# A two-layer mixer in one kernel: Newton's steps on GpSimd, two weight loads moved ahead, block sums moved back

## The chip, the cores and the metric

The kernel runs on one core of a Trainium2 chip. Its engines are TensorE (PE in the profile; its weight loads are PEld), VectorE (DVE), ScalarE (ACT), GpSimd (POOL) and SyncE (SP), which issues most of the DMAs. Each engine works through its own queue in order, and semaphores tie the queues together. The metric is the device time of one execution in microseconds (us); three runs are shown, and the execution that was profiled has a time of its own.

## The reference

```python
D_MODEL, SEQ, CHUNK = 1024, 512, 64          # batch 1, float32, 8 heads of 128
# layer 0: gated linear recurrence (HGRN2) and squared-ReLU MLP; then a shared K/V projection
# layer 1: differential attention over that K/V and squared-ReLU MLP
def rms_norm(x, w):
    y = xf * lax.rsqrt(jnp.mean(xf * xf, axis=-1, keepdims=True) + EPS)
    return (y * w).astype(x.dtype)
def hgrn2_mixer(h, w_in, lb, gate_norm_w, w_out):        # h is rms_norm(x, a_norm_pre)
    proj = h @ w_in
    q, f, i, g = jnp.split(proj, ...)                    # 1024 columns each
    ...                                                  # q, k and log_f from q and f, per head
    o = hgrn2_recurrence(q, k, log_f, i)                 # chunks of 64 frames
    o = rms_norm(o, gate_norm_w) * jax.nn.silu(g)
    return o.reshape(B, S, D_MODEL) @ w_out
```

All that the change touches lies in the HGRN2 mixer, the first 290 us of 1271: the statistics 1/rms of x (512 numbers), the projections q and f (per head), i (the "values") and g (the "gates"), the recurrence, the norm of each head's output and the projection by `w_out`.

## The kernel before

Activations lie transposed, features on the 128 partitions and 512 frames along the row. Every large product is made of three matmuls in a short format: an operand is split into `hi` (a rounded copy, made by ACT) and `lo` (the rest, made by DVE as raw minus hi), and PE adds hi·hi, hi·lo and lo·hi. So each weight block passes through a DMA into a `raw` buffer (tag `raw`, 4 buffers), an ACT copy (`whi_…`) and a DVE subtraction (`wlo_…`; 8 buffers each) before PE can use it. In the tiles' names `qf` is a head's q and f columns, `wi`/`i` the first half of the values, `wg`/`g` the first pair of gates, `gs` and `is` the later gates and values, which are computed from sums of blocks (seven products in place of eight), `ao` the output projection.

`split_w` does the splitting with ACT and DVE. `split_d` leaves DVE out: ACT writes hi and minus raw, and a DMA issued by POOL adds the raw weights onto the latter in memory (`accum_op`), so `wlo` then comes from a DMA. Heads 0 to 3 take the first way (`load_w`), heads 4 to 7 the second (`load_d`).

The statistics: ACT squares x (`sqx`), DVE adds the four squares, PE sums over the partitions (`ps_mc`, 16 small matmuls), and `rsqrt_col` makes 1/sqrt of the 128x4 result `rcol`: `nx` = mean + eps, a first guess by integer arithmetic, and three Newton steps of three instructions each on tiles of 128x4 (`nt`, `rcol`). Then `nrcol`, the diagonal matrix `dg`, and PE's product `ps_sp`, which spreads the 512 numbers over the partitions; DVE copies it to `rb`, with which every gate is scaled. Head 0 and head 1 wait for `rb`.

`block_sums` makes four sums and differences of halves of the normalised input (tiles `sums`, then `whi_x`, `wlo_x`, and the last into `uhi`, `ulo`), which the later gates and values need (first at `gs_x`, 116 us). Its first step is eight ACT copies of x, scaled, into `sums` (L720), each 128x256.

The first projections follow one another on PE: head 0's and head 1's q and f, the values (`i`, four tiles of 512 columns), the first gates (`g`), heads 2 and 3, and so on. `head` runs beside them: gates, then seven levels of the recurrence, in which two to four heads alternate between a few small matmuls (`gl`), DVE multiplications (L849, L850) and a masked copy (L825), then state (`st`), output (`o`), `head_norm` (squares, `rsqrt_col`, scaling into `os_a`, four transposes `hn_a` on PE) and `store_u`.

What sets the order: PE's queue is the order in which the Python generators issue its instructions. `Plan` keeps a planned time, which each matmul advances; a chain such as `head` yields planned delays (the `W_…` numbers: `W_HEAD` between a head's norm and its transposes) or conditions, and is resumed when these are over; the main chain fills the time between. The queues of the other engines are arranged by the framework's scheduler by what is ready and by priority, within the dependences; `tc.issue_after` holds instructions behind a given one.

Of the kernel before, what the change touches and what calls it, by code (L numbers as in the profile page):

```python
# [13 lines left out]
AF = mybir.ActivationFunctionType  # L14
# [3 lines left out]
P = 128  # L18
# [15 lines left out]
W_KEYS, W_STATE = 1.5, 0.8  # L34
W_HEAD, W_STORE = 11.7, 5.5
W_QK, W_NEXT, W_P, W_PER_TILE, W_PT = 3.6, 0.94, 5.0, 0.66, 2.5
# [52 lines left out]
def trunk_kernel(ctx: ExitStack, tc: tile.TileContext, x_t, w_qf, w_g, w_gs, w_i, w_is, w_ao, w_kv, w_q, w_bo, w_up, w_us, w_dn,  # L89
# [73 lines left out]

    last_split = []

# [37 lines left out]

    def load_d(src, ncols, name):

        out = []
        per = 1024 // ncols
        for pr in range(ncols // 128):
            out += split_d(fetch_w(src, ncols, pr, name), src[:, per * pr:per * (pr + 1), :], f"{name}_{pr}")
        return out  # L210
# [28 lines left out]

    def rsqrt_col(ms, add, out, scale=1.0):  # L240

        n = ms.shape[1]
        x = cp.tile([P, 4], F32, tag="nx", name="nx", bufs=4)[:, :n]
        t = cp.tile([P, 4], F32, tag="nt", name="nt", bufs=4)[:, :n]
        if isinstance(add, float):
            v.tensor_scalar(x, ms, scale, add, op0=ALU.mult, op1=ALU.add)
        else:
            v.scalar_tensor_tensor(x, ms, scale, add, op0=ALU.mult, op1=ALU.add)
        v.tensor_scalar(out.bitcast(I32), x.bitcast(I32), -0.5, 1597463007.0, op0=ALU.mult, op1=ALU.add)
        for _ in range(3):  # L250
            v.scalar_tensor_tensor(t, out, -0.5, out, op0=ALU.mult, op1=ALU.mult)
            v.tensor_tensor(t, t, x, op=ALU.mult)
            v.scalar_tensor_tensor(out, t, 1.5, out, op0=ALU.add, op1=ALU.mult)

# [366 lines left out]

    def head_norm(pool, po, add, name):

# [6 lines left out]
        for c in range(4):  # L630
            if c % 2 == 0:
                v.tensor_scalar(os[:, c, :], po[:, c * P:(c + 1) * P], y[:, c:c + 1], None, op0=ALU.mult)
            else:
                a.activation(os[:, c, :], po[:, c * P:(c + 1) * P], AF.Copy, scale=y[:, c:c + 1])
        yield W_HEAD
        pt = smt(f"hn_{name}")
# [58 lines left out]
    def block_sums(xs, ts):  # L695

        gain = gn[:, G_APRE:G_APRE + 8]
        e, f = sums

        def split(src, sign, n):  # L700
            if n < 3:
# [16 lines left out]
        for r in range(4):  # L718
            for n, t in enumerate((e, f)):
                a.activation(t[:, r], xs[2 * r][:, n * 256:n * 256 + 256], AF.Copy, scale=gain[:, 2 * r:2 * r + 1])  # L720
            yield 2.0
        v.tensor_tensor(e, e, f, op=ALU.subtract)
        split(e, 1.0, 0)
        yield 5.0
        odd(1, f, ALU.subtract)
        split(f, 1.0, 1)
        yield 5.0
        odd(1, e, ALU.add)
        split(e, -1.0, 2)
        yield 5.0  # L730
        odd(0, e, ALU.subtract)
        split(e, -1.0, 3)

    def start(hp, xs, maskf):
# [14 lines left out]
        yield W_XSUM  # L749
        rsqrt_col(mean_cols([ssum[:, j, :] for j in range(2)], S, onesd), EPS, rcol)  # L750
        v.tensor_scalar(nrcol, rcol, -1.0, None, op0=ALU.mult)
# [40 lines left out]
    def hgrn(hp, w0, xs):  # L792
# [8 lines left out]
        def head(h, pss):  # L801
            if h < 2:
# [10 lines left out]
                            tf.rearrange("p (c t) -> p c t", c=4), op=ALU.mult)  # L813
            a.activation(qc[:, :, P:192], qq.rearrange("p (c b two) -> p c b two", c=4, two=2)[:, :, :, 1], AF.Copy)
            yield W_GATE if h >= 2 else W_GATE_FIRST
# [74 lines left out]
            done(("po", h))  # L890
            for pt in head_norm(hp, po, EPS, f"a{h}"):
                if isinstance(pt, float):
                    yield pt
# [131 lines left out]
        for p in range(4):  # L1025
            for h in (2 * p, 2 * p + 1):
                if h >= 3 and h % 2:
                    yield until(("rec", h - 3))
                wt = w0 if h == 0 else w1 if h == 1 else load_w(w_qf[h], 256, None, f"qf{h}") if h < 4 else load_d(w_qf[h], 256, f"qf{h}")
                pss = [mmt(f"qf{h}_{n}") for n in range(2)]  # L1030
# [13 lines left out]
            if p == 0:  # L1044
                wv = load_w(w_i, 512, None, "wi")
                vts[0], vts[1] = [hp.tile([P, 4, 256], F32, tag="vt", name=f"vt{i}", bufs=3) for i in range(2)]
                for tt in range(4):

                    ps = (smt if tt < 2 else mmt)(f"i{tt}")
                    for kt in range(8):  # L1050
                        xmm(ps, wv, kt, 512, tt * P, kt == 0, kt == 7)
                        yield 0
                    if tt == 0:
                        yield until("rcol")
                    for i in range(2):
                        a.activation(vts[i][:, tt, :], ps[:, i * 256:(i + 1) * 256], AF.Copy, scale=rcol[:, tt:tt + 1])
                yield until("rb")
                spawn(block_sums(xs, ts), 2.0)
                wt = load_w(w_g, 256, None, "wg")
                for j in range(2):  # L1060
# [48 lines left out]
    def attention(ap, f):  # L1109
# [27 lines left out]
        def unit(h, qi, kq, vt, bt, po, mx):  # L1137
# [40 lines left out]
            if qi == 3:  # L1178

                ez = col("ez")  # L1180
                v.scalar_tensor_tensor(ez, mx[:, :, 2], EPS, mx[:, :, 2], op0=ALU.mult, op1=ALU.mult)
                for hn in head_norm(ap, po, ez, f"b{h}"):
                    if isinstance(hn, float):
                        yield hn
                store_u(h, hn)
                yield W_STORE
                done(("amix", h))
# [166 lines left out]
```

## Time and profile before

| | |
|---|---|
| three runs | 1271.01, 1273.31, 1273.58 us; median 1273.31 |
| the profiled execution | 1273.18 us, span on the core 1271.4 us |
| PE busy | 1240.0 us, 98% of the span |
| DVE, ACT, POOL busy | 825.8, 673.9, 95.6 us |
| DMA | 158.54 MB, mean 125 GB/s |
| chain that ended last | PE 79%, DMA 6%, issue 6%, DVE 5%, ACT 4% |

A page of the profile gives busy time by engine, then the span in slices, the DMA queues, the chain that ended last, and the costliest groups of instructions. The sum of the prediction is made against the profiled execution, 1273.18 us, which lies 0.13 us under the median. With PE at 98%, what is to be read is where PE stands still, and for whom.

### The profile page before, as it was taken

The numbers are of one execution on the slowest core, as the hardware profiler recorded it, in microseconds if no ns is written. First come the engines' busy times: TensorE is split into PE (matmuls) and PEld (weight loads), VectorE is DVE, ScalarE is ACT, GpSimd is POOL, SyncE is SP. The second block draws the span as 40 slices with busy tenths as digits, with TensorE's granted clock in tenths as the row PEclk, the third lists the DMA queues.
The fourth block names the chain that finished last, engine by engine and source line by source line (L and its number), as shares of the span: only waits on it lengthen the run. The fifth ranks groups of instructions, "written<-read, shape, count | busy, mean of one in ns | idle before, by whom it ended". The sixth has DMA issues, their size and how long they took to land.

```text
span 1271.4 us, 21443 instructions
## 1 busy us (share of the span) xinstructions
PE 1240.0 (98%) x8440; PEld 1122.8 (88%) x8440; DVE 825.8 (65%) x1654; ACT 673.9 (53%) x1248; POOL 95.6 (8%) x166
## 2 busy tenths in 40 slices
PE   9999999999999999999999999999999999999996
PEld 7788898899988988989999787889998898988996
DVE  7768885866854654636488978664885463663645
ACT  7345546437751733715556877664773371561632
POOL 0102211210000000000100000001000000000000
PEclk9999999999999999999999999999999999999999
DMA  7223557342356663644616322313435355363521
GB/s 253 72 67 92 122 115 184 94 150 68 135 166 124 179 149 95 186 106 115 217 51 203 113 88 79 100 63 105 137 111 158 96 175 122 103 196 74 158 102 67
DMA packets 57303, 158.54 MB, mean 125 GB/s; under 512 B 6354, under 2 KB 8659, under 8 KB 57203
## 3 DMA queue, kind: packets, MB, share of 16 engines
q1 hardware_dynamic: 45920, 120.34, 30.2%
q0 software_dynamic: 11040, 36.71, 13.7%
q8 instruction: 66, 1.08, 0.4%
q14 instruction: 35, 0.28, 0.1%
q10 hardware_dynamic: 242, 0.13, 0.0%
HBM read 147.45 MB, written 9.70 MB: 124 GB/s over the span
## 4 chain that ended last, share of the span: by engine, by line
PE 79%; issue 6%; DMA 6%; DVE 5%; ACT 4%; POOL 0%; SPq 0%; DVEq 0%; ACTq 0%; POOLq 0%
PE dn L114 20%; PE qf L114 7%; PE up L114 7%; PE ux L114 6%; PE kq L114 6%; PE ao_h L114 3%; DMA raw_s<-in_w_us_dram 3%; PE bo_h L114 3%; PE dn_h L114 3%; PE uz L114 3%; PE gl L114 3%; PE v L114 3%; PE g L114 2%; PE lg L114 2%; PE i L114 2%
## 5 line engine op out<-in xcount | busy, mean ns | idle before, releaser
L114 PE MATMUL dn<-uhi,whi_dn 128*128 128x512 f32 x384 | 151.9, 396 | 0.0
L114 PE MATMUL dn<-ulo,whi_dn 128*128 128x512 f32 x384 | 151.9, 396 | 0.0
L114 PE MATMUL dn<-uhi,wlo_dn 128*128 128x512 f32 x384 | 151.9, 395 | 0.0
L200 ACT ACTIVATE whi_a<-raw_a 128x1024 fp32r<-128x1024 f32 x24 | 25.4, 1059 | 118.5 <-PE dn L114 115.6
L114 PEld LDWEIGHTS dn<-uhi,whi_dn 128*128 128x128 f32 x384 | 72.2, 188 | 17.8 <-ACT r L563 0.7
L114 PEld LDWEIGHTS dn<-uhi,wlo_dn 128*128 128x128 f32 x384 | 72.2, 188 | 17.3
L114 PEld LDWEIGHTS dn<-ulo,whi_dn 128*128 128x128 f32 x384 | 72.2, 188 | 16.9
L173 DVE TENSOR_TENSOR wlo_dn<-raw_dn,whi_dn 128x1024 fp32r<-128x1024 f32 x64 | 76.6, 1220 | 5.9 <-ACT whi_dn L172 4.6
L468 DVE TENSOR_TENSOR ulo<-r,uhi 128x1024 fp32r<-128x1024 f32 (+1 forms) x40 | 40.2, 1010 | 53.7 <-ACT uhi L467 53.7
L114 PE MATMUL up<-xhi,wlo_up 128*128 128x256 f32 x256 | 72.1, 281 | 1.0 <-DVE wlo_up L173 1.0
L114 PE MATMUL up<-xhi,whi_up 128*128 128x256 f32 x256 | 72.6, 284 | 0.0
L114 PE MATMUL up<-xlo,whi_up 128*128 128x256 f32 x256 | 71.8, 281 | 0.0
L172 ACT ACTIVATE whi_dn<-raw_dn 128x1024 fp32r<-128x1024 f32 x64 | 65.7, 1051 | 7.1 <-PE up L114 3.0
L114 PE MATMUL dn_h<-uhi,whi_dn 128*128 128x256 f32 x240 | 66.6, 278 | 0.0
L114 PE MATMUL dn_h<-ulo,whi_dn 128*128 128x256 f32 x240 | 66.3, 276 | 0.0
L114 PE MATMUL dn_h<-uhi,wlo_dn 128*128 128x256 f32 x240 | 66.3, 276 | 0.0
L610 DVE TENSOR_TENSOR zacc<-dn,zacc 128x512 f32<-128x512 f32 x32 | 22.1, 691 | 59.1 <-PE dn L114 59.0
L512 POOL DMA_DIRECT2D raw_s<-in_w_us_dram x24 | 20.8, 866 | 490.3 <-DMA raw_s<-in_w_us_dram 288.3
L114 PE MATMUL qf<-xhi,whi_qf 128*128 128x512 f32 x128 | 53.2, 415 | 1.7 <-ACT xhi L679 1.4
L114 PE MATMUL qf<-xhi,wlo_qf 128*128 128x512 f32 x128 | 51.4, 402 | 1.8 <-DMA wlo_qf<-in_w_qf_dram 1.7
L114 PE MATMUL qf<-xlo,whi_qf 128*128 128x512 f32 x128 | 51.4, 401 | 0.3 <-DVE xlo L680 0.3
L200 ACT ACTIVATE whi_t<-raw_a 128x1024 fp32r<-128x1024 f32 x24 | 25.5, 1061 | 49.4 <-PE dn L114 27.2
(531 smaller groups left out, 4133.8 us busy)
## 6 DMA issues: line engine op xcount, KB each, us to landing
raw_dn<-in_w_dn_dram SPq DMA_DIRECT2D x64, 512.0 KB, 4.5
raw_a<-in_w_us_dram SPq DMA_DIRECT2D x24, 512.0 KB, 4.3
raw_s<-in_w_us_dram SPq DMA_DIRECT2D x48, 256.0 KB, 4.4
raw_s<-in_w_us_dram POOLq DMA_DIRECT2D x24, 512.0 KB, 6.4
raw_up<-in_w_up_dram SPq DMA_DIRECT2D x16, 512.0 KB, 4.2
raw_wkv<-in_w_kv_dram SPq DMA_DIRECT2D x16, 512.0 KB, 3.7
raw_qf<-in_w_qf_dram SPq DMA_DIRECT2D x14, 512.0 KB, 4.8
raw_d<-in_w_us_dram SPq DMA_DIRECT2D x12, 512.0 KB, 4.3
```

Of the source, the lines that this page charges most:

```text
L114: nc.tensor.matmul(out, lhsT, rhs, **kw)
L172: last_split[:] = [a.activation(hi, raw, AF.Copy)]
L173: v.tensor_tensor(lo, raw, hi.bitcast(F32), op=ALU.subtract)
L200: a.activation(hi, raw, AF.Copy)
L468: v.tensor_tensor(ulo[pr][:, :, lo:hi], r, uhi[pr][:, :, lo:hi].bitcast(F32), op=ALU.subtract)
L512: g.dma_start(rs, ws[p, :, 0:2, :], accum_op=ALU.add)
L610: v.tensor_tensor(z, pss[n4], z, op=ALU.add)
```

## The change

It has six edits, all in the mixer.

- `rsqrt_col` gets `aside`. For x's statistics alone the three Newton steps go from DVE to POOL, as four instructions a step (twelve in place of nine).
- The first gates' weights `wg` and head 2's weights are loaded before the values' loop is issued, right behind `wi`. Before, `wg` was asked for after the values and head 2's when its turn came; the queues' order for these DMAs is the same before and after.
- `block_sums` is started by head 1 instead of the main chain; its eight ACT copies stand behind head 1's `qc` copy, and the rest behind the last evicted tile of the values (`done("i")`, `marks`).
- Heads 6 and 7 are split by ACT and DVE (`load_w`); heads 4 and 5 stay with the DMA (`split_halves`).
- The transposes of the last head's norm are planned 9.0 after it in place of 11.7 (`W_HEAD_LAST`).
- `copies` is made a function of its own.

```diff
-W_HEAD, W_STORE = 11.7, 5.5
+W_HEAD, W_HEAD_LAST, W_STORE = 11.7, 9.0, 5.5
...
-    def load_d(src, ncols, name):
+    def split_halves(src, name, aside):
+        if not aside:
+            return load_w(src, 256, None, name)
         out = []
...
-    def rsqrt_col(ms, add, out, scale=1.0):
+    def rsqrt_col(ms, add, out, scale=1.0, aside=False):
...
         for _ in range(3):
-            v.scalar_tensor_tensor(t, out, -0.5, out, op0=ALU.mult, op1=ALU.mult)
-            v.tensor_tensor(t, t, x, op=ALU.mult)
-            v.scalar_tensor_tensor(out, t, 1.5, out, op0=ALU.add, op1=ALU.mult)
+            if aside:
+                g.tensor_tensor(t, out, out, op=ALU.mult)
+                g.tensor_tensor(t, t, x, op=ALU.mult)
+                g.tensor_scalar(t, t, -0.5, 1.5, op0=ALU.mult, op1=ALU.add)
+                g.tensor_tensor(out, out, t, op=ALU.mult)
+            else:
+                ...
...
-        yield W_HEAD
+        yield W_HEAD_LAST if last else W_HEAD
...                                                     # block_sums
         for r in range(4):
-            for n, t in enumerate((e, f)):
-                a.activation(t[:, r], xs[2 * r][:, n * 256:n * 256 + 256], AF.Copy, scale=gain[:, 2 * r:2 * r + 1])
+            with tc.issue_after(marks["a"].ins):
+                copies(r)
             yield 2.0
         v.tensor_tensor(e, e, f, op=ALU.subtract)
-        split(e, 1.0, 0)
-        yield 5.0
-        ...
+        yield until("i")
+        for n in range(4):
+            with tc.issue_after(marks["i"].ins):
+                ...
+            yield 3.0
...
+            if h == 1:
+                marks["a"] = odd
+                spawn(block_sums(xs, ts), W_GATE_FIRST)
...
-                wt = w0 if h == 0 else w1 if h == 1 else load_w(w_qf[h], 256, None, f"qf{h}") if h < 4 else load_d(w_qf[h], 256, f"qf{h}")
+                wt = w0 if h == 0 else w1 if h == 1 else w2 if h == 2 else split_halves(w_qf[h], f"qf{h}", h in (4, 5))
...
                 wv = load_w(w_i, 512, None, "wi")
+                wt = load_w(w_g, 256, None, "wg")
+                w2 = load_w(w_qf[2], 256, None, "qf2")
...
                 yield until("rb")
-                spawn(block_sums(xs, ts), 2.0)
-                wt = load_w(w_g, 256, None, "wg")
```

What it moves on the engines, at three places. The first is the head of ACT's queue, where x and head 0's weights are split as they arrive (`xraw`, `raw_qf`). Before:

```order
L741 ACTIVATE lbe<-lbe 128x8
L720 ACTIVATE sums_82<-xraw_74,gn 128x256
L720 ACTIVATE sums_83<-xraw_74,gn 128x256
L679 ACTIVATE xhi_66<-xraw_74,gn 128x512
L659 ACTIVATE whi_qf_0_129<-raw_qf_0_127 128x512
L679 ACTIVATE xhi_66<-xraw_74,gn 128x512
L659 ACTIVATE whi_qf_0_129<-raw_qf_0_127 128x512
L720 ACTIVATE sums_82<-xraw_75,gn 128x256
L720 ACTIVATE sums_83<-xraw_75,gn 128x256
L679 ACTIVATE xhi_67<-xraw_75,gn 128x512 x2
```

And now:

```order
L751 ACTIVATE lbe<-lbe 128x8
L686 ACTIVATE xhi_66<-xraw_74,gn 128x512
L666 ACTIVATE whi_qf_0_129<-raw_qf_0_127 128x512
L686 ACTIVATE xhi_66<-xraw_74,gn 128x512
L666 ACTIVATE whi_qf_0_129<-raw_qf_0_127 128x512
L686 ACTIVATE xhi_67<-xraw_75,gn 128x512 x2
```

The eight copies of the block sums have left the start; they stand behind head 1's `qc` copy and the second evicted tile of the values.

The second place is DVE's queue from the mean (`nx`) to `rb`. Before, Newton's steps (`nt`, `rcol`) stand between the splits of the values', gates' and head 2's weights and the block sums; twelve rows of it, with `nrcol`, `dg` and `rb` ten rows further on:

```order
L246 TENSOR_SCALAR nx<-ps_mc 128x4
L173 TENSOR_TENSOR wlo_wi_347<-raw_wi_344,whi_wi_346 128x1024
L249 TENSOR_SCALAR rcol<-nx 128x4
L173 TENSOR_TENSOR wlo_wg_596<-raw_wg_593,whi_wg_595 128x1024
L251 SCALAR_TENSOR_TENSOR nt<-rcol 128x4
L173 TENSOR_TENSOR wlo_wg_602<-raw_wg_599,whi_wg_601 128x1024
L252 TENSOR_TENSOR nt<-nt,nx 128x4
L707 TENSOR_TENSOR wlo_x_716<-sums_82,whi_x_715 128x1024
L253 SCALAR_TENSOR_TENSOR rcol<-nt,rcol 128x4
L173 TENSOR_TENSOR wlo_qf_0_727<-raw_qf_0_724,whi_qf_0_726 128x1024
L251 SCALAR_TENSOR_TENSOR nt<-rcol 128x4
L715 SCALAR_TENSOR_TENSOR sums_82<-xraw_74,gn,sums_82 128x256
```

And now, from `nx` to head 2's second split:

```order
L247 TENSOR_SCALAR nx<-ps_mc 128x4
L173 TENSOR_TENSOR wlo_wi_344<-raw_wi_341,whi_wi_343 128x1024
L250 TENSOR_SCALAR rcol<-nx 128x4
L173 TENSOR_TENSOR wlo_wi_350<-raw_wi_347,whi_wi_349 128x1024
L173 TENSOR_TENSOR wlo_wg_356<-raw_wg_353,whi_wg_355 128x1024
L761 TENSOR_SCALAR nrcol<-rcol 128x4
L765 TENSOR_TENSOR dg<-ident,rcol 128x512
L173 TENSOR_TENSOR wlo_wg_362<-raw_wg_359,whi_wg_361 128x1024
L173 TENSOR_TENSOR wlo_qf_0_368<-raw_qf_0_365,whi_qf_0_367 128x1024
L769 COPY rb<-ps_sp 128x512
L173 TENSOR_TENSOR wlo_qf_1_374<-raw_qf_1_371,whi_qf_1_373 128x1024
```

Nine Newton instructions have gone to POOL, where twelve now open the queue; `nrcol` waits for POOL's last one. One more split of the values stands behind `nx`, and head 2's second split has come up to `rb` from the levels of heads 0 and 1.

The third place is DVE's queue at the end of the third pair of gates (`gs`, the tiles g), just ahead of head 6's projection. Before:

```order
L201 TENSOR_TENSOR wlo_tgs_1925<-raw_ags_1902,whi_tgs_1924 128x1024
L948 TENSOR_TENSOR g_1931<-gs_y,g_1931 128x256
L952 TENSOR_TENSOR g_1931<-gs_z,g_1931 128x256
L936 TENSOR_TENSOR g_1931<-g_1931,rb 128x512
L955 TENSOR_TENSOR g_1932<-gs_x,g_1932 128x256
L941 TENSOR_TENSOR g_1931<-g_1931,egs_2004 128x512
```

And now:

```order
L201 TENSOR_TENSOR wlo_tgs_1928<-raw_ags_1905,whi_tgs_1927 128x1024
L173 TENSOR_TENSOR wlo_qf_0_2044<-raw_qf_0_2041,whi_qf_0_2043 128x1024
L961 TENSOR_TENSOR g_1934<-gs_y,g_1934 128x256
L173 TENSOR_TENSOR wlo_qf_1_2050<-raw_qf_1_2047,whi_qf_1_2049 128x1024
L965 TENSOR_TENSOR g_1934<-gs_z,g_1934 128x256
L949 TENSOR_TENSOR g_1934<-g_1934,rb 128x512
L173 TENSOR_TENSOR wlo_qf_0_2200<-raw_qf_0_2197,whi_qf_0_2199 128x1024
L954 TENSOR_TENSOR g_1934<-g_1934,egs_2007 128x512
L968 TENSOR_TENSOR g_1935<-gs_x,g_1935 128x256
L173 TENSOR_TENSOR wlo_qf_1_2206<-raw_qf_1_2203,whi_qf_1_2205 128x1024
```

The four low halves of heads 6 and 7 have come to DVE; the four DMAs that made them have left POOL's queue, and ACT makes four copies fewer. On PE the order is the same to the row, but for one piece: the last head's four transposes `hn_a` stand three matmuls of `ao_h` earlier.

39 lines of the change are left out of this document (21 added, 18 removed).

## Prediction

> **What bounds the kernel now.** I read the page first. Its first line gives the span and its part 1 the busy time of each engine:
>
> ```profile
> span 1271.4 us, 21443 instructions
> PE 1240.0 (98%) x8440; PEld 1122.8 (88%) x8440; DVE 825.8 (65%) x1654; ACT 673.9 (53%) x1248; POOL 95.6 (8%) x166
> ```
>
> PE is the bound nearly throughout. The change removes no matmul and reorders only one group, so it can gain only where PE stands still or runs at a lower clock. The view of waits for PE (who waited for whom: us in total, times, longest) gives the stops inside the stretch that the change touches:
>
> ```profile
> PE ps_sp L114 <- DVE dg L755: 3.0, 1, 3.0
> PE qf L114 <- DMA wlo_qf<-in_w_qf_dram: 1.7, 1, 1.7
> PE ao_h L114 <- ACT uhi L643: 1.4, 1, 1.4
> PE qf L114 <- ACT xhi L679: 1.4, 1, 1.4
> PE qf L114 <- DVE xlo L680: 0.3, 1, 0.3
> ```
>
> Then I asked for the clock in stretches of 3.41 us, with edges where the granted clock (PEclk) is seen to change. The columns are the stretch, its length, PE's busy time, the clock, and the share and rate of DMA:
>
> ```profile
> 9.32:12.73 3.41, 1.75 (x7) 1.00 1.07 393
> 12.73:16.15 3.42, 3.42 (x9) 0.50 1.01 400
> 36.63:40.04 3.41, 0.44 (x2) 1.00 0.76 246
> 40.04:43.45 3.41, 3.34 (x6) 0.50 0.23 87
> 207.29:210.71 3.42, 1.69 (x12) 1.00 1.07 250
> 210.71:214.12 3.41, 3.41 (x23) 1.00 1.04 248
> 285.80:289.21 3.41, 1.62 (x12) 1.00 0.00 0
> 289.21:292.63 3.42, 3.42 (x19) 0.50 0.00 0
> ```
>
> Three of the four stops are paid twice: the wait, and then a stretch at half clock, in which 3.41 x 0.5 = 1.71 us of work is lost. The stretch with 1.69 us busy was not punished and the one with 1.75 was, so the border lies about there and is not sharp. The Trainium skill ("TensorE: Matmul & The Clock Gate", Part 1 and the table under "Why this matters for your kernels") says that the window is 3413 ns long and free-running, and that gaps under about 3 us keep the clock. The trace agrees on the length (3.41 us); on the gap it does not, since a wait of 1.4 us beside one of 0.3 halved the clock here, and the trace decides. By the rule the first clock term below would be nothing and the sum 1.71 us smaller.
>
> **A: the block sums' copies leave ACT's start.** PE's first long wait and ACT's rows before it:
>
> ```profile
> 11.17 0.51 PE L114 MATMUL qf<-xhi,whi_qf 128*128 128x512 f32 x1 [1.38 <-ACT xhi L679]
> 9.60 0.91 ACT L720 ACTIVATE sums<-xraw,gn 128x256 f32<-128x256 f32 x2 [0.75 <-DMA xraw<-in_x_t_dram]
> 10.41 1.32 ACT L679 ACTIVATE xhi<-xraw,gn 128x512 fp32r<-128x512 f32 x2
> 26.77 1.22 DVE L692 TENSOR_TENSOR sqx<-sqx,sqx 128x1024 f32<-128x1024 f32 x1
> 28.07 1.93 PE L114 MATMUL ps_mc<-onesd,sqx 128*128 128x1 f32 x16
> ```
>
> ACT was waiting for x and then made two copies for the block sums before the split on which PE waits. Without them the split starts at 9.60 in place of 10.41: 0.81 us. The wait falls to 0.57 us and the small one for `xlo` stays, so PE is busy some 2.56 us of that stretch, farther from 1.75 than from full; I take the half clock as gone, 1.71 us. PE then reaches `ps_mc` 2.5 us earlier, at 25.6. The sum that it needs ended at 27.99 (26.77 + 1.22) and must be earlier too: ACT is rid of eight copies at 0.45 (0.91 for two), 3.6 us, ahead of its last square, so it should end about 24.5. A is 0.81 + 1.71 = 2.52 us.
>
> **B: Newton's steps on POOL.** Call T the end of `ps_mc`, 28.07 + 1.93 = 30.0 before. The rows on the way to `ps_sp`, then POOL's and DVE's small instructions:
>
> ```profile
> 30.03 0.16 DVE L246 TENSOR_SCALAR nx<-ps_mc 128x4 f32<-128x4 f32 x1 [0.90 <-PE ps_mc L114]
> 31.25 0.16 DVE L249 TENSOR_SCALAR rcol<-nx 128x4 int32<-128x4 int32 x1
> 39.37 0.68 DVE L755 TENSOR_TENSOR dg<-ident,rcol 128x512 f32<-128x512 f32 x1
> 40.11 1.22 PE L114 MATMUL ps_sp<-dg,ones 128*128 128x512 f32 x1 [3.04 <-DVE dg L755]
> 51.79 0.48 POOL L853 TENSOR_TENSOR tt<-tt 128x8 f32<-128x8 f32 x2
> 236.30 1.19 POOL L853 TENSOR_TENSOR tt<-tt 128x64 f32<-128x64 f32 x1
> 236.11 1.23 DVE L201 TENSOR_TENSOR wlo_tgs<-raw_ags,whi_tgs 128x1024 fp32r<-128x1024 f32 x1 [1.06 <-ACT whi_tgs L200]
> 95.15 0.16 DVE L251 SCALAR_TENSOR_TENSOR nt<-yh 128x4 f32<-128x4 f32 x1
> 95.34 0.16 DVE L252 TENSOR_TENSOR nt<-nt,nx 128x4 f32<-128x4 f32 x1
> ```
>
> Before, `dg` starts 8.1 us behind the first guess `rcol`, though nine steps at DVE's spacing of 0.19 to 0.20 (95.34 - 95.15) are 1.8 us: the rest is other work standing between them. Now `rcol` ends at T + 1.4 as before (one split stands ahead of it, as then), and POOL starts at T + 1.5. Two dependent small POOL instructions take 0.48 together, the last of them 0.20, so 0.28 a step when DVE is quiet. When DVE runs a large subtraction POOL's instruction lasts until it ends: the POOL row at 236.30 ends at 237.49, the DVE row at 237.34. In the new order two such subtractions stand behind `rcol` (the last of `wi`, the first of `wg`), from T + 1.3 to T + 3.7; in them two steps get done, and then DVE waits at `nrcol` and the other ten run at 0.28. That ends at T + 6.6, `nrcol` adds about 0.1 (an estimate: half of a DVE step of 0.2) and `dg` 0.74 to PE's start as before (39.37 to 40.11), so `ps_sp` can start at T + 7.45. Bounds: all twelve at 0.28 give T + 5.7, all twelve held to 1.19 T + 16.6, and six of each T + 11.2. I take T + 7.45, near the lower end, since DVE has nothing to run once it waits at `nrcol`.
>
> PE comes there at T + 7.07 (40.11 - 3.04), in place of a start at T + 10.11. The wait is 0.4 in place of 3.04, the gain 2.66 us, and a stretch with 0.4 us idle does not halve the clock: 1.71. B is 4.37 us. The Trainium skill ("GPSIMD Engine Reference", 4.1 Engine selection) says the opposite of this edit: elementwise work belongs on VectorE, GpSimd being about twice as slow. On the single step the rows agree (0.28 and twelve, against 0.20 and nine: 3.4 us against 1.8); by that rule alone the path would grow by 1.6 us and the time would be 1270.2. It leaves out DVE's queue, which is what the 8.1 us are made of.
>
> What the wait delays: behind `nrcol` DVE holds the second split of `wg` and the first of head 2 (1.2 each), then `rb`, then head 2's second split, then the gates of heads 0 and 1. `rb` stands about as far behind `ps_sp` as before, the gates one split (1.2 us) farther, and PE, no longer at half clock, comes 1.7 us sooner to the first products of the two heads: 2.9 us of their cover go. How much there was:
>
> ```profile
> 50.46 0.43 ACT L814 ACTIVATE qc<-q 128x256 f32<-128x256 f32 x1 [1.83 <-DVE q L812]
> 53.66 2.76 PE L114 MATMUL g<-qc,k 128*128 128x192 f32 x16
> ```
>
> Head 1's last operand was there at 50.89, 2.8 us before PE began on head 0's products, and its own stand in the second half of that row, 1.4 us later: 4.2 us. That leaves 1.3, so I charge nothing; should the weights of head 2 come late, up to 2 us.
>
> **The moved block sums.** Eight ACT copies go to a place where ACT waited for PE, and DVE's subtraction and first four `sums` products (1.2 and 1.7 us) come from the start into the levels of heads 0 and 1; head 2's second split (1.2) leaves them. What the levels have to spare:
>
> ```profile
> 61.70 0.84 ACT L1056 ACTIVATE vt<-i,rcol 128x256 f32<-128x256 f32 x2 [9.06 <-PE i L114]
> 54.50:79.50 25.00, 19.85 (x48) 1.00 0.07 23
> 60.67 0.42 DVE L850 TENSOR_TENSOR k<-k,tt 128x256 f32<-128x256 f32 x1
> 63.08 0.54 PE L114 MATMUL gl<-q,k 128*124 128x64 f32 x4
> ```
>
> DVE is busy 19.85 of 25 us there, and about 1.7 us come in on balance. A level's last product ends at 61.09 and PE takes it at 63.08: 2.0 us, into which one inserted piece of 1.2 fits. I charge 0; bounds 0 and 2 us. The loads ahead cost nothing either: their DMA order is unchanged.
>
> **C: heads 6 and 7 split by DVE.** PE waits for head 6's low half, which a POOL DMA completes; DVE has holes just there:
>
> ```profile
> 210.43 0.50 PE L114 MATMUL qf<-xhi,wlo_qf 128*128 128x512 f32 x1 [1.73 <-DMA wlo_qf<-in_w_qf_dram]
> 202.74 0.42 DVE L948 TENSOR_TENSOR g<-gs_y,g 128x256 f32<-128x256 f32 x1 [2.42 <-PE gs_y L114]
> ```
>
> On DVE the same half takes 1.2 us (a subtraction of 128x1024, as the row at 236.11) in the hole of 2.42 us before 202.74, 6 us before PE asks for it (210.43 - 1.73). Three more halves, 3.7 us, come behind it and put off only the gates' own additions, which no product of PE waits for soon. C is 1.73 us; the four DMAs fewer only help.
>
> **D: the last head's transposes.** They move up by three matmuls, which start 0.11 apart there, 0.34 us; their input was ready long before:
>
> ```profile
> 282.73 0.37 ACT L634 ACTIVATE os_a<-o,yh 128x128 f32<-128x128 f32 x1 [0.42 <-DVE os_a L632]
> 285.64 0.60 PE L119 MATMUL hn_a<-ident,os_a 128*128 128x128 f32 x4
> 287.68 0.39 PE L114 MATMUL ao_h<-uhi,whi_ao 128*128 128x256 f32 x1 [1.45 <-ACT uhi L643]
> ```
>
> The scaled output is there at 283.10. So D is 0.34 us, and the stretch is then busy 1.96 us. Whether that keeps the clock is between 0 and 1.71 us; 1.96 is nearest the 1.62 to 1.75 of the rows, two of which were punished, so I take 0 and leave 1.71 to the range.
>
> **The sum.** 2.52 + 4.37 + 1.73 + 0.34 = 8.96 us. From the profiled execution's 1273.18 that is 1264.2.
>
> **The rivals.**
> - *POOL is slow at Newton's steps.* With six steps held, at T + 11.2, `ps_sp` starts 1.1 later than before and the half clock stays: 2.52 + 1.73 + 0.34 - 1.1 = 3.5, so 1269.7. For it: the 1.19 us of a POOL row beside DVE. Against: DVE waits meanwhile. 12 in 100, with the cases on the way to it. With all twelve held it would be 1275.1, which nothing in DVE's new order can bring about.
> - *Newton's path grows by its own steps*, as by the Trainium skill's rule: 3.4 - 1.8 = 1.6 us later with the half clock kept, 2.52 + 1.73 + 0.34 - 1.6 = 3.0, or 1270.2. Against: the 8.1 us. 4 in 100.
> - *The cover of the first gates is gone*: 2 us, 1266.2. For it: three splits now stand between `dg` and the gates. 7 in 100; it lies in the range.
> - *The levels wait for DVE* (the other side). PE has 14 groups of level products and transposes for heads 0 and 1, and each would wait for a product that DVE holds behind a piece of the block sums. From 8.96 / 14 = 0.64 us a group the gain is eaten; at 1 us a group the time is 1278.2. Against: 2.0 us to spare at a level and 1.7 us added to 5.1 us of idle time. 4 in 100, and 4 for half of it, 1271.2.
> - *The forecast, with D's clock kept*: 1262.5; about a third of the forecast's chance.
>
> **How the numbers follow.** The forecast with both outcomes of D keeps 69 in 100. Two tenths of a per cent, 2.5 us, is about what can be told from no change here. Faster than 1270.8 are the forecast, POOL's case, the rule's and the gates': 69 + 12 + 4 + 7 = 0.92; within, the half case of the levels, 0.04; above 1275.9 their whole case, 0.04. The range goes from a little under D's better outcome, 1262.0, to 1269.0, short of POOL's case; some 0.8 lies in it.
>
> **What would show it.** Right: the wait before `ps_sp` under 1 us and the clock at 1.00 from 12 to 45 us; twelve POOL rows in about 5 us; `xhi` at 9.6; no wait at head 6; `hn_a` three matmuls up. Wrong: POOL steps over 0.5 us with DVE idle, gaps before `gl` from 45 to 75 us, or PE late at the first gates of heads 0 and 1.

## The result and the profile after

Four executions of the changed kernel took 1259.38 to 1262.88 us, median 1260.31, against 1273.44 for the kernel before beside them: ratio 0.9901, 95% interval 0.9879 to 0.9923. The profiled execution took 1259.98 us, 13.20 less than that of before. The direction was forecast; the time lies 3.9 us under the 1264.2 that was predicted and 1.7 under the low end of the range. In two later comparisons (below) the same kernel had medians of 1263.57 and 1262.94, ratios 0.9927 (0.9910 to 0.9944) and 0.9921 (0.9904 to 0.9939). The median of all 16 executions is 1262.86.

The page after, and the waits of PE (us in total, times, longest):

```profile
span 1258.1 us, 21436 instructions
PE 1234.5 (98%) x8440; PEld 1119.2 (89%) x8440; DVE 828.9 (66%) x1649; ACT 669.9 (53%) x1244; POOL 96.0 (8%) x174
```
```profile
PE ux L114 <- DVE r L565: 1.3, 3, 0.5
PE ao_h L114 <- ACT uhi L650: 1.1, 1, 1.1
PE qf L114 <- ACT xhi L686: 0.6, 1, 0.6
PE ps_sp L114 <- DVE dg L765: 0.3, 1, 0.3
```

PE has 5.5 us less of busy time with the same 8440 matmuls, and 5.1 of them are the clock: three stretches of 3.41 us ran at half clock before, and after none does until 1251 us, when PE is done. The wait for `dg` is 0.3 in place of 3.0, the wait for head 6's low half is gone, and the first long wait has halved. `ux`, of which the prediction said nothing, stood at 3.9 us in 5 waits before:

```profile
PE ux L114 <- DVE r L558: 3.9, 5, 1.1
```

The rows of the profile after (start, duration, engine and line, what is computed, and in brackets the idle time before it and its releaser) that answer to those of the prediction, with `up`, the next product behind the change, in both kernels:

```profile
9.66 1.33 ACT L686 ACTIVATE xhi<-xraw,gn 128x512 fp32r<-128x512 f32 x2 [0.72 <-DMA xraw<-in_x_t_dram]
10.43 0.50 PE L114 MATMUL qf<-xhi,whi_qf 128*128 128x512 f32 x1 [0.62 <-ACT xhi L686]
27.66 0.16 DVE L247 TENSOR_SCALAR nx<-ps_mc 128x4 f32<-128x4 f32 x1 [1.68 <-PE ps_mc L114]
29.14 1.10 POOL L253 TENSOR_TENSOR nt<-rcol 128x4 f32<-128x4 f32 x1 [28.68 <-DVE rcol L250]
30.32 1.05 POOL L254 TENSOR_TENSOR nt<-nt,nx 128x4 f32<-128x4 f32 x1
31.47 0.19 POOL L255 TENSOR_SCALAR nt<-nt 128x4 f32<-128x4 f32 x1
33.97 0.20 POOL L256 TENSOR_TENSOR rcol<-rcol,nt 128x4 f32<-128x4 f32 x1
35.02 0.70 PE L114 MATMUL ps_sp<-dg,ones 128*128 128x512 f32 x1 [0.32 <-DVE dg L765]
278.69 0.39 PE L114 MATMUL ao_h<-uhi,whi_ao 128*128 128x256 f32 x1 [1.09 <-ACT uhi L650]
307.77 0.39 PE L114 MATMUL up<-xhi,wlo_up 128*128 128x256 f32 x1 [0.50 <-DVE wlo_up L173]
```
```profile
318.38 0.38 PE L114 MATMUL up<-xhi,wlo_up 128*128 128x256 f32 x1 [0.49 <-DVE wlo_up L173]
```

Read from place to place, the gain is 287.68 - 278.69 = 8.99 us at `ao_h`, the last step of the change; 10.61 at `up`, 30 us later; and 13.3 at the end. So the four terms of the prediction (8.96) came out to 0.03 us in sum. Then 1.6 us came behind `ao_h`, where before had a stretch at half clock and after has none. The last 2.7 us came behind `up`, where the waits at `ux` in the MLPs fell by 2.6 and where no line of the MLPs was changed. (One edit reaches further than the mixer: the last head of layer 1's attention is planned at 9.0 too. But PE's order of 8440 matmuls is the same in both kernels except at `ao_h`.) The experiments ask what the 1.6 and the 2.7 us are.

### The profile page after: what moved, and what is told of

It reads as the page before. It is cut to its first block, busy times and chain, and to the rows that moved or that the text cites. A ratio compares the mean times of both kernels' runs of the same rounds, so it can differ in the third digit from the quotient of the medians.

```text
span 1258.1 us, 21436 instructions
## 1 busy us (share of the span) xinstructions
PE 1234.5 (98%) x8440; PEld 1119.2 (89%) x8440; DVE 828.9 (66%) x1649; ACT 669.9 (53%) x1244; POOL 96.0 (8%) x174
## 4 chain that ended last, share of the span: by engine, by line
PE 87%; DVE 5%; ACT 3%; DMA 3%; issue 2%; POOL 0%; SPq 0%; DVEq 0%; ACTq 0%
PE dn L114 21%; PE ux L114 9%; PE up L114 7%; PE qf L114 7%; PE kq L114 6%; PE dn_h L114 5%; PE uz L114 4%; PE bo_h L114 3%; PE ao_h L114 3%; PE gl L114 3%; PE v L114 2%; PE g L114 2%; PE uy L114 2%; PE i L114 2%; PE lg L114 2%
```

## The experiments

Each comparison has its own executions of the kernel before: medians 1273.10, 1272.81 and 1273.48 us.

**The changed kernel again, twice (no edit).** The first, in the first comparison:

> The changed kernel once more, unaltered. Of the 13.2 us between the two profiles some 10.6 are the terms of the prediction and some 2.7 lie in the two MLPs, which the change does not touch: PE's waits at the products ux for DVE's r were 3.9 us in 5 stops before and are 1.3 us in 3 stops after. Theory (chance): each of these stops hangs on one DMA that POOL issues to add two weight blocks in memory (raw_s), which took 6.3 to 8.0 us to land in the two profiles; then a second profile of the same kernel has another sum of these waits, anywhere from 0.5 to 4 us and at other places, and the time moves with it, 1259 to 1263 us. Rival (the change moved the phase of the queues): 1.2 to 1.4 us at the same three places, 420, 589 and 1183 us.

Measured: 1263.57 us (1261.72 to 1264.14). The profiled execution took 1264.14; three of PE's waits, DVE's row behind one of them, and two stretches of the clock. The columns of such rows are here and below the stretch, its length, the busy time of PE, PEld, DVE, ACT and POOL with the number of instructions, the clock, and the share and rate of DMA:

```profile
PE ux L114 <- DVE r L565: 2.0, 4, 1.0
PE qf L114 <- ACT xhi L686: 1.3, 1, 1.3
PE gl L114 <- DVE yh L250: 1.1, 1, 1.1
```
```profile
138.86 1.23 DVE L991 TENSOR_TENSOR raw_tis<-raw_tis,raw_ais 128x1024 f32<-128x1024 f32 x1 [2.64 <-DMA raw_tis<-in_w_is_dram]
```
```profile
8.26:11.67 3.41, 1.84 (x7) 0.95 (x7) 1.62 (x3) 2.31 (x4) 0.00 (x0) 1.00 1.05 403
11.67:15.08 3.41, 3.41 (x9) 2.67 (x10) 3.34 (x6) 3.02 (x6) 0.00 (x0) 0.50 1.05 395
```

This execution is 4.2 us longer than the first profile, and four things account for it: 0.7 in the first wait (x's blocks landed later), 1.7 in a stretch at half clock behind it, 1.1 where DVE stood for a load (`raw_tis`) with the `yh` queued behind that a level's product waits for, and 0.7 at `ux`. The same kernel, then, with other landings. The second, in the second comparison:

> The changed kernel unaltered, as the measure for the other three and as another draw. Theory (chance in DMA landings and in where the stretches of the clock fall): its time lies anywhere from 1260 to 1264 us, the waits at ux sum to 1 to 5 us and differ from 1.3 and 2.0, and the profiles' difference is accounted for by the first wait, a halved stretch or none, the wait at 140 us for DVE's yh (0 or up to 1.2) and ux. Rival (the two chips differ throughout): every matmul stretch of the slower one is longer by the same share.

Measured: 1262.94 us (1260.53 to 1264.78). The profiled execution, 1263.31 us, has no halved stretch, and 4.4 us in 6 waits at `ux`, 3.1 of the 3.3 us by which it exceeds the first. That leaves nearly nothing for the rival, a slower chip. What DVE's `r` stood behind is seen in the rows of the queues from 1167 us (SPq is SyncE's queue of DMAs):

```profile
1167.60 0.55 SPq L514 DMA_DIRECT2D raw_a<-in_w_us_dram  x1
1171.11 0.82 SPq L518 DMA_DIRECT2D raw_s<-in_w_us_dram  x2
1176.14 0.86 POOL L519 DMA_DIRECT2D raw_s<-in_w_us_dram  x1 [25.40 <-DVE raw_a L528]
1183.55 1.06 ACT L200 ACTIVATE whi_s<-raw_s 128x1024 fp32r<-128x1024 f32 x1 [2.38 <-DMA raw_s<-in_w_us_dram]
1184.64 1.23 DVE L201 TENSOR_TENSOR wlo_s<-raw_s,whi_s 128x1024 fp32r<-128x1024 f32 x1 [1.64 <-ACT whi_s L200]
1185.78 0.42 DVE L565 TENSOR_TENSOR r<-ux,p 128x256 f32<-128x256 f32 x1
1186.25 0.39 PE L114 MATMUL ux<-xhi,whi_d 128*128 128x256 f32 x1 [0.54 <-DVE r L565]
```

PE is released by `r`, and `r` had no wait of its own: it stands behind the split `wlo_s`, that behind ACT's `whi_s`, and that behind POOL's adding DMA, 7.4 us after its issue. The view of waits names the last link; the first is a DMA. Over the 24 of these DMAs of this execution the landing took 5.4 to 8.1 us, and 5.3 to 8.9 over the ten profiles with this code unaltered. In the ten the waits at `ux` sum to 1.3, 2.0, 2.3, 2.6, 3.2, 3.8, 3.9, 4.4, 5.1 and 5.2 us, whichever parts of the change are in, and the first profile after has the least of them. Theory "chance" holds. The rival falls: in the second profile the waits are at 423, 508, 1102 and 1187 us, and not at the first one's 420, 589 and 1183 alone.

**The loads of raw_s asked for ahead.**

```diff
+                if p % 2 == 0:
                     ra = raw("a"); nc.sync.dma_start(ra, ...)
                 rs = raw("s"); ...
                 g.dma_start(rs, ws[p, :, 0:2, :], accum_op=ALU.add)
+                if p % 2:
+                    ra = raw("a"); nc.sync.dma_start(ra, ...)
```

> The changed kernel with one thing altered in code that the change does not touch: in the MLPs, for odd pairs of blocks, the load of raw_s (completed by POOL's adding DMA, 6 to 8 us to land) is asked for ahead of raw_a, and so gets the buffer that comes free 4 us sooner. Theory (PE's waits at ux for DVE's r are that adding DMA's landing, different in each execution: 3.9 us in all in one profile of before; 1.3, 2.0, 3.2, 5.2 and 2.6 in those of the changed kernel and its variants): the waits at ux fall under 0.5 us in all, and the time is 1.5 to 3 us under the changed kernel's in this comparison, with a smaller spread. Rival (these waits come from PE's own progress, the evictions or DVE's queue, and the DMA only ends last by chance; or raw_a is late in its place): no change in the time, and waits of 1 to 5 us at ux remain.

Measured: 1257.41 us (1256.93 to 1259.43), 5.5 us under the changed kernel of the same comparison; ratio to before 0.9882 (0.9861 to 0.9902). PE's waits at `ux` are gone from the view. The same place of the program, now at 1163 us. Below it is one entry each of what ended ACT's idle time before `whi_s` (us, times): first with the loads ahead, where PE's `dn` and `uz` are all there is, then in the changed kernel's profile beside it, where the DMA is an entry too:

```profile
1163.22 0.81 SPq L519 DMA_DIRECT2D raw_s<-in_w_us_dram  x2
1167.11 0.56 SPq L523 DMA_DIRECT2D raw_a<-in_w_us_dram  x1
1168.18 0.86 POOL L520 DMA_DIRECT2D raw_s<-in_w_us_dram  x1 [21.55 <-DVE r L557]
1177.11 1.06 ACT L200 ACTIVATE whi_s<-raw_s 128x1024 fp32r<-128x1024 f32 x1 [0.26 <-PE uz L114]
```
```profile
  PE uz L114: 3.3, 12
```
```profile
  DMA raw_s<-in_w_us_dram: 12.3, 5
```

Measured from `raw_d`, the load ahead of both (1160.21 here, 1164.58 there), the adding DMA is issued 3.6 us earlier and lands at 1175.49, before ACT comes to it, though it takes no less time (6.1 to 8.4 us over the 24). The theory holds and the rival falls: the load was what these waits ended on. The gain is above the 1.5 to 3 us expected, and above the 4.4 us in the view. Read from place to place, PE needs 942.3 us from the `up` product named above to its last matmul in the changed kernel's profile and 936.2 in this one: 6.0 us less, nearly all of it in steps at the `ux` products, so these stops cost more than the idle time that the view lists. This version beats both kernels. Once more, in the third comparison:

> The changed kernel with raw_s asked for ahead of raw_a, once more, as the measure for its neighbours here. Theory: about 1257.4 us again, no wait at ux over 0.3 us, and a spread of the executions of under 3 us. Rival (1257.4 was a favourable draw): 1260 or more.

Measured: 1258.06 us (1257.21 to 1258.67), ratio 0.9877 (0.9858 to 0.9896); five executions within 1.5 us, and again no wait at `ux` in the view. The rival falls.

**The kernel before with the same alteration** (the diff above, in the kernel before):

> The kernel before with the same alteration of the MLPs' loads (raw_s asked for ahead of raw_a in odd pairs), nothing of the change in it. With the waits at ux gone from both, the difference to the changed kernel with that alteration is the change's own, freed of the largest term that varies from one execution to the next. Theory (the sum of the prediction, 8.96 us, plus the clock behind the last head's wait, which the prediction took as 0 and which is 1.71 us in those executions whose stretch covers the wait): 9 to 10.7 us between the two. Rival (part of the first 13 us was a lasting effect of the change on the MLPs): 11 us or more.

Measured: 1268.40 us (1265.96 to 1270.41), ratio 0.9961 (0.9948 to 0.9974). With the waits at `ux` out of both, the change is worth 1268.40 - 1258.06 = 10.3 us: the sum of 8.96 and most of a halved stretch. The medians alone leave about 1 us of doubt on that, and so the rival's 11 us open (an estimate from the spread of the executions). The traces decide: from `up` to its last matmul PE needs 935.5 us here and 936.2 and 936.8 in the two profiles of the changed kernel with the loads ahead. With the loads as they were it is 941.9 and 942.6 in the kernel before and 939.2, 940.3 and 942.3 in the changed kernel, and over all ten such profiles 939.2 to 943.7, the first profile after being the shortest. So nothing lasting came to the MLPs with the change, and the first comparison's 13.1 us held about 2.8 of chance.

**Newton's steps back on DVE.**

```diff
-        rsqrt_col(mean_cols(...), EPS, rcol, aside=True)
+        rsqrt_col(mean_cols(...), EPS, rcol)
```

> The changed kernel with Newton's nine steps back on DVE; all else as changed. The block sums are gone from DVE's queue there, and between rcol and nrcol stand four splits of 1.25 us in place of eight large pieces. By the prediction's working nine steps of 0.20 and four splits of 1.25 end at T + 8.2 (T the end of ps_mc, 27.6), dg and the product follow at T + 9.2 in place of T + 7.4: 1.8 us more wait before ps_sp, 2.1 in all, and with 1.3 us busy a stretch at half clock, 1.7: 1260.3 + 3.5 = 1263.8; 1262.1 if the clock stays. Rival 1 (the gain at ps_sp came from the block sums' leaving DVE, POOL's steps are no faster): within 0.5 us of 1260.3. Rival 2 (the whole of term B, 4.37, is POOL's): 1264.7.

Measured: 1266.10 us (1263.57 to 1266.89), 2.5 more than the changed kernel in the same comparison. Some of DVE's rows from the first guess on, and PE's:

```profile
28.71 0.16 DVE L250 TENSOR_SCALAR rcol<-nx 128x4 int32<-128x4 int32 x1
29.92 0.16 DVE L258 SCALAR_TENSOR_TENSOR nt<-rcol 128x4 f32<-128x4 f32 x1
29.99 1.22 DVE L173 TENSOR_TENSOR wlo_wg<-raw_wg,whi_wg 128x1024 fp32r<-128x1024 f32 x1
33.94 0.16 DVE L260 SCALAR_TENSOR_TENSOR rcol<-nt,rcol 128x4 f32<-128x4 f32 x1
34.86 1.23 DVE L173 TENSOR_TENSOR wlo_qf<-raw_qf,whi_qf 128x1024 fp32r<-128x1024 f32 x1 [0.77 <-ACT whi_qf L172]
36.07 0.68 DVE L765 TENSOR_TENSOR dg<-ident,rcol 128x512 f32<-128x512 f32 x1
```
```profile
36.81 0.70 PE L114 MATMUL ps_sp<-dg,ones 128*128 128x512 f32 x1 [2.27 <-DVE dg L765]
```

The steps themselves take 0.16 us, 0.20 from one to the next; four splits of 1.22 stand between the first guess and `dg`, and the wait is 2.27 (2.1 expected). Against the 0.32 with POOL that is 2.0 us, so rival 1 falls, and so does rival 2, which had it at 4.37. In this profile an edge of the stretches at 35.92 cut the wait in two, and the clock was kept. By the Trainium skill ("GPSIMD Engine Reference", 4.1 Engine selection) the work should have stayed on VectorE. Here that is the slower place by 2.0 us, since the other engine's queue was empty.

**Newton's steps on POOL alone**, in the kernel before:

```diff
+            if aside:
+                ...                          # the changed kernel's four instructions a step
-        rsqrt_col(mean_cols(...), EPS, rcol)
+        rsqrt_col(mean_cols(...), EPS, rcol, aside=True)
```

> The kernel before with one part of the change alone: Newton's twelve steps on POOL (term B without the block sums' move). DVE has the same pieces between nx and dg as in the changed kernel. Theory of the prediction: ps_sp starts at T + 7.4 in place of T + 10.1, the wait falls from 3.04 us to about 0.3, and the stretch there is not halved: 2.7 + 1.7 = 4.4 us, 1268.8 from 1273.2 (1270.5 if the clock was kept before in most executions). Rival (the way to ps_sp was long because of the block sums on DVE, and POOL's steps are no shorter): wait above 2 us, time within 1 us of before.

Measured: 1268.56 us (1267.36 to 1271.69), ratio 0.9971 (0.9959 to 0.9983), 4.2 us under before. PE:

```profile
37.26 0.70 PE L114 MATMUL ps_sp<-dg,ones 128*128 128x512 f32 x1 [0.32 <-DVE dg L761]
```

Term B needs none of the other parts. But with the block sums away from DVE already, POOL adds only 2.5: some 0.8 of the old wait (3.04 against 2.27) were the block sums'. Beyond the wait POOL brought 1.5 us alone and 0.5 there. That fits a wait of 2.27 us being cut by an edge, and so keeping the clock, more often than one of 3.04; with one profile of each version it is not shown.

**The block sums as before.**

```diff
-            with tc.issue_after(marks["a"].ins):
-                copies(r)
+            ...                              # the eight copies at the start, pieces not held behind the values
-                spawn(block_sums(xs, ts), W_GATE_FIRST)     # in head 1
+                spawn(block_sums(xs, ts), 2.0)              # in the main chain, behind rb
```

> The changed kernel with the block sums as before: the eight ACT copies at the start, DVE's pieces not held behind the values. Newton stays on POOL. Theory (term A): PE's first long wait grows by 0.8 us, and in executions whose stretch holds all of it the clock is halved, 1.7 more: 0.8 to 2.5 us slower than the changed kernel in this comparison; ps_sp still waits 0.3 us. Rival (the levels of heads 0 and 1 pay for the moved sums in the changed kernel, so undoing them gains there what it loses at the start): within 0.5 us of the changed kernel, with the first wait 0.8 longer and less elsewhere.

Measured: 1266.13 us (1264.15 to 1268.45), 3.2 above the changed kernel of the same comparison, where term A is 2.52 and 0.8 to 2.5 was expected. In the profile the first wait is 2.02 us, and `ps_mc` waits 0.72 for DVE's sum of squares. The prediction saw that this sum ends earlier without the copies, but gave it no price. The halved stretch lay behind `ps_mc` here and not behind the first wait (its rows stand in the last section). Against the changed kernel's profile beside it PE is 4.7 us behind at 35 us and 4.6 at `up`, so the levels gain nothing back: the rival falls.

**Heads 6 and 7 by POOL's DMA again.**

```diff
-... split_halves(w_qf[h], f"qf{h}", h in (4, 5))
+... split_halves(w_qf[h], f"qf{h}", h >= 4)
```

> The changed kernel with heads 6 and 7 split by ACT and POOL's DMA again. Theory of the prediction: the wait of 1.73 us for head 6's low half comes back and nothing else, 1262.0 us; with a halved stretch behind it 1263.7. Rival (the DMA is hidden now that the start is 10 us shorter, or DVE's four pieces cost as much elsewhere): 1260.3 within 0.5.

Measured: 1265.53 us (1264.59 to 1267.32), 2.0 above the changed kernel beside it, so the rival falls. The wait is back, to the tenth, with no halved stretch behind it:

```profile
PE qf L114 <- DMA wlo_qf<-in_w_qf_dram: 1.7, 1, 1.7
```

**The last head's transposes at 11.7 again.**

```diff
-W_HEAD, W_HEAD_LAST, W_STORE = 11.7, 9.0, 5.5
+W_HEAD, W_HEAD_LAST, W_STORE = 11.7, 11.7, 5.5
```

> The changed kernel with the last head's transposes planned at 11.7 again, so that hn_a stands three matmuls later. The wait before ao_h, 1.09 us in the changed kernel, must be about 1.43 and the time 0.34 longer. The profile before had a halved stretch behind this wait (1.62 us busy of 3.41), the profile after had none (about 1.98 busy). Theory (the three matmuls kept the clock): a halved stretch of 3.41 us comes back, 1.71 + 0.34 = 2.05, 1262.4 us. Rival (where the free-running stretches fall relative to the wait decides, not the three matmuls): no halved stretch, 1260.65 us, or one in some executions only.

Measured: 1262.03 us (1260.60 to 1264.72). The executions are 4.1 us apart and its neighbour's 2.4, so the time tells nothing of 0.34 us; the profile does: the wait is 1.44 in place of 1.09. No stretch was halved behind it. So the rival holds in this execution, and where the stretches lie has to be read beside the wait.

**The kernel before again (no edit).**

> The kernel before, unaltered, for a second profile. Theory (which stops are punished by half clock depends on where the free-running stretches of 3.41 us fall): other stops than the three of the first profile may be halved, from none to four, while the waits themselves (1.4 before the first xhi or thereabouts, 3.0 before ps_sp, 1.7 for head 6, 1.45 and 0.34 before ao_h) stay; the waits at ux sum to something other than 3.9 us. Rival (each stop has its fixed price): the same three stretches, behind the same three waits.

Measured: 1274.62 us, one execution; 5.1 us at `ux`, 1.6 at the first wait, and the waits before `ps_sp`, at head 6 and before `ao_h` as before. Three stretches are halved again, but not the same three: one behind the first wait, none behind `ao_h`'s, and two in succession behind `ps_sp`'s, which an edge at 39.41 cuts:

```profile
39.41:42.82 3.41, 2.50 (x4) 1.37 (x5) 1.21 (x4) 0.00 (x0) 0.00 (x0) 0.50 0.48 169
42.82:46.24 3.42, 3.42 (x10) 2.65 (x9) 3.39 (x7) 2.36 (x5) 0.06 (x1) 0.50 0.00 0
```

So the rival, a fixed price for each stop, falls. Now the stretches that hold PE's waits before `ao_h`, and the ones behind them; where no clock changes nearby, the edges are counted in steps of 3.41 us from a change elsewhere in the same trace. First the kernel before, second profile; then Newton alone; then the transposes at 11.7; then the changed kernel with raw_s ahead:

```profile
288.58:292.00 3.42, 1.91 (x14) 1.71 (x15) 1.70 (x4) 2.48 (x3) 0.00 (x0) 1.00 0.01 0
292.00:295.41 3.41, 3.41 (x32) 3.41 (x30) 0.87 (x2) 3.36 (x8) 0.00 (x0) 1.00 0.02 5
```
```profile
280.96:284.37 3.41, 1.62 (x12) 1.19 (x11) 1.57 (x3) 1.55 (x2) 0.00 (x0) 1.00 0.00 0
284.37:287.78 3.41, 3.41 (x17) 3.41 (x18) 0.27 (x1) 1.89 (x4) 0.00 (x0) 0.50 0.00 0
```
```profile
278.45:281.86 3.41, 2.36 (x18) 2.16 (x19) 1.16 (x3) 2.91 (x4) 0.00 (x0) 1.00 0.00 0
```
```profile
278.05:281.47 3.42, 1.99 (x15) 1.59 (x14) 1.85 (x4) 1.91 (x2) 0.00 (x0) 1.00 0.00 0
281.47:284.88 3.41, 3.41 (x32) 3.41 (x32) 0.69 (x1) 3.32 (x7) 0.00 (x0) 1.00 0.02 5
```

The waits of 1.45 and 0.34 are the same in the first three. In the first an edge at 288.58 leaves the wait's first 0.3 us (from 288.30) in the stretch before, 1.91 us stay busy, and the clock is kept; in the second all of it lies in one stretch, 1.62 stay busy, and the next runs at half clock, as in the first profile of before; in the third an edge at 278.45 cuts the wait in its middle. In the fourth, with the transposes three matmuls up, both waits lie whole in one stretch, and 1.99 us keep the clock. The other profiles say the same: where both waits lie whole in one stretch, the clock was halved in all three with the transposes at 11.7 and kept in all three at 9.0, and in the eight in which an edge cuts them it was kept. The Trainium skill ("TensorE: Matmul & The Clock Gate", Part 1) calls the window free-running and its effect different from run to run; that agrees with these edges. The rule of the same page's table ("Why this matters for your kernels"), by which gaps of this length keep the clock, does not.

**The values' first block split by DVE**, on top of raw_s ahead:

```diff
-            a11, = split_d(ra, w_is[:, 0:1, :], f"a11{nm}")
+            a11, = split_b(ra, f"a11{nm}")
```

> The same altered kernel, and besides the values' first block (a11) is split by ACT and DVE and not by POOL's adding DMA. In the changed kernel DVE's addition raw_tis waits 0.1 to 2.8 us for a load that takes 7.4 to 9.9 us to land while that adding DMA runs beside it, and PE's gl behind it waits 0 to 1.3 us for DVE's yh near 140 us. Theory (the two transfers hold each other up): the load lands in 4 to 5 us, the wait for yh is gone, 0.3 to 1.3 us faster than the unaltered neighbour. Rival (the load is late whatever runs beside it, or DVE's added 1.2 us are paid in the levels): no gain or up to 1.2 us slower, with waits of PE at gl remaining.

Measured: 1257.94 us (1257.57 to 1259.67) beside 1258.06: no difference. The load `raw_tis` still took 8.3 us to land (9.0 in the neighbour) without the adding DMA of `a11` beside it, so that one was not what held it. Two other adding DMAs, of head 5's low halves, still ran beside it (issued at 124.51 and 127.47 us, landed at 132.34 and 136.15, the load from 127.20 to 135.53); whether these hold it was not tried. PE's wait for `yh` (0.2 in the neighbour) is gone all the same: DVE's order is another one with the added split, and it comes to `raw_tis` when the load is there. It is worth no more than the 0.2 here. Why this load is slow stays open.

## Why the prediction was right, and where it was not

The sum gave 8.96 us, and the two profiles' spans differ by 13.3. Of the 4.3 us between, 1.6 are the clock behind `ao_h`, which the prediction took as 0 (D), and 2.7 lie behind `up`, where the sum has no term at all. The first alone would have left the time at 1262.5, inside the range; the second put it outside.

- **A** (2.52): `xhi` at 9.66 as said (9.60), `ps_mc` ended 2.4 us earlier (`nx` at 27.66 against 30.03; 2.5 forecast). Undone, it cost 3.2 us. Right, but no part of it is a fixed size. The changed kernel's first wait was 0.62, 1.29 and 0.95 us in its three profiles, and behind the one of 1.29 the clock was halved; of the five profiles with the copies at the start three were halved there, of the nine without them one. That the four terms came out to 0.03 us is closer than this wait repeats, and so in part luck. The reason given for the clock was misread too: 2.56 us busy are not farther from 1.75 than from a full 3.41 (0.81 against 0.85). 2.51 were measured there, and kept the clock.
- **B** (4.37): right in each step. `ps_sp` started at T + 7.4 (T + 7.45 forecast), two POOL steps were held beside DVE's subtractions (1.10 and 1.05), ten ran at 0.28, the wait was 0.32. Alone it measured 4.2. Behind the wait of 3.04 the clock was halved in all three profiles that have it, and behind the shorter ones in none of eleven. The terms of A and B share a piece, though: 2.5 of B is left once the block sums are gone.
- **C** (1.73): right, 2.0 undone. The gates' additions, put off by three more halves, made nobody wait.
- **D** (0.34): the matmuls right, 1.44 against 1.09. **D's clock is the term that was mis-sized**: taken as 0, it was 1.6 us between the two profiles. The prediction set 1.96 us busy nearest to the punished 1.62 to 1.75; it is on the other side, 1.99 and 1.91 keep the clock. In the profile after itself, though, the shorter stop does not lie in one stretch at all. An edge at 278.61 cuts it (the two rows below the list). The longer stop, so cut, kept the clock too with the transposes at 11.7 again (edge at 278.45), so this profile alone does not show what the three matmuls did; the three with 1.99 or 1.98 us busy do. It is also no fixed price: in the kernel before, the waits before `ao_h` and the matmul between them span 2.2 us, which leaves (3.4 - 2.2) / 3.4, about a third of the positions, in which one stretch covers them (an estimate from these rows; it was three of the five profiles with the transposes at 11.7). The case "D's clock kept", 1262.5, is the one that happened; all 16 executions together have 1262.86.
- **The range** failed by what it left out: **the waits at `ux` were put at nothing, without a reason**. The low end of 1262.0 had D's clock in it and nothing for the MLPs, which the change leaves alone. The view of waits showed 3.9 us at `ux`, and the three runs shown were 2.6 us apart. That those waits hang on a DMA with 5.3 to 8.0 us to land could have been asked of the trace of before; that their sum differs from 1.3 to 5.2 us took ten profiles to see. A range for one comparison of a few runs needed 2 to 3 us on each side for it. The first comparison's executions are the shortest of the three; with the other two the median lies inside the range, by 0.9 us, so the miss is in part the luck of that draw. Only one of those first four was profiled, so that the others were short for the same reason is not shown.
- **The rivals** of the prediction fell: POOL was not held for six steps and the path did not grow by its own (0.32 us of wait), the first gates and the levels of heads 0 and 1 never made PE wait, as one row shows (PE busy in all of 45 to 75 us in the profile after, DVE in 24.85 of 30):

```profile
45.00:75.00 30.00, 30.00 (x193) 25.93 (x192) 24.85 (x60) 9.42 (x21) 3.12 (x11) 1.00 0.00 1
```

The two loads moved ahead were not undone alone. The prediction gave them nothing, and SyncE's 286 DMAs do stand in the same order in both kernels. The stretches at `ao_h` in the profile after:

```profile
275.19:278.61 3.42, 2.41 (x22) 2.20 (x20) 0.69 (x1) 0.60 (x1) 0.00 (x0) 1.00 0.03 11
278.61:282.02 3.41, 2.99 (x23) 2.79 (x24) 1.17 (x3) 2.94 (x6) 0.00 (x0) 1.00 0.00 0
```

## What to carry to other kernels

A chain of small dependent instructions is slow because of what is queued between its steps: count the large pieces there, and where they take longer than the dearer steps would, move the chain to an engine with an empty queue. Where a view of waits names an engine that had no wait of its own, follow its queue back to the first instruction that did: here that was a DMA, and asking for it one buffer earlier gave 5.1 to 5.5 us in three comparisons, more than any one part of the change. Before a few microseconds are put down to an edit, take a second profile of the same kernel and sum the waits in the code that it leaves alone.

## What the runs showed of the hardware

- The price of a stop of PE between about 1.4 and 2.3 us depends on where the free-running stretches of 3.41 us cut it: the same 1.45 + 0.34 us cost 1.7 us more or nothing. There is no single border in PE's busy time: 1.62, 1.75 and 1.84 were punished, 1.69 to 1.75 at head 6's wait (four profiles) and 1.91 before `ao_h` were not. And busy time in the records is not all that counts: with the block sums as before this stretch, which holds the 16 one-column matmuls of `ps_mc`, was punished with 2.69 us busy, in the one profile of that version.

```profile
27.92:31.33 3.41, 2.69 (x20) 2.37 (x20) 2.51 (x4) 2.12 (x2) 0.00 (x0) 1.00 0.70 221
31.33:34.74 3.41, 3.41 (x10) 2.64 (x9) 2.83 (x4) 1.06 (x1) 2.16 (x4) 0.50 0.78 267
```

- A small POOL instruction of 0.20 us lasted 1.10 and 1.05 us beside DVE's subtractions of two operands in memory. The Trainium skill ("SBUF — State Buffer", Who interferes with whom) gives the reason, a read interface that both share; the rows agree.
- A DMA that adds 512 KB in memory took 5.3 to 8.9 us to land in ten profiles, and which of 24 was slow changed from one execution to the next.
